# Down stages' first loads in another order, and three neighbours: a kernel for one encoder layer

## The chip, the cores and the metric

The kernel runs on one core of a Trainium2 chip. The metric is the time of one execution on the device in microseconds, as the median of several runs. TensorE (PE) multiplies matrices, VectorE (DVE), ScalarE (ACT) and GpSimd (POOL) work element by element, and SyncE (SP) issues most DMA transfers; ACT issues some as well. Each engine runs its instructions strictly in order: one that waits holds up all that stand behind it on that engine, DMA issues included.

## The reference

One layer of a post-norm encoder is applied to two groups of requests (256 and 512 tokens of 1024 features, 768 tokens in all) with the same weights, in float32:

```python
def swiglu(x, w_gu, w_down):
    gate, up = jnp.split(x @ w_gu, 2, axis=-1)
    return (jax.nn.silu(gate) * up) @ w_down
...
x = layer_norm(DN_ALPHA * x + 0.5 * swiglu(x, ffn1_w_gu[l], ffn1_w_down[l]), ln_g[l, 0], ln_b[l, 0])
x = layer_norm(DN_ALPHA * x + parallel_mixer(...), ln_g[l, 1], ln_b[l, 1])
x = layer_norm(DN_ALPHA * x + memory_cross_attention(x, mem, xa_w_q[l], xa_w_kv[l], xa_w_o[l]), ln_g[l, 2], ln_b[l, 2])
x = layer_norm(DN_ALPHA * x + 0.5 * swiglu(x, ffn2_w_gu[l], ffn2_w_down[l]), ln_g[l, 3], ln_b[l, 3])
```

The hidden width of the two feed-forward layers is 2816. The mixer is a short convolution beside a gated linear attention; the cross-attention reads 256 memory tokens per group, from which it makes keys and values (`k, v = jnp.split(mem @ w_kv, 2, axis=-1)`).

## The kernel before

**Products in three parts.** Each operand of a matrix product is split into a high and a low half (`split`, lines 86 to 88): ACT makes the high half by a conversion (L87, `wh` of a weight tile), DVE or POOL the low one by subtracting it (L88, `wl`). Three matmuls then stand for one: high by high, high by low, low by high. A weight tile so passes through a load into `raw`, a conversion on ACT and a subtraction on DVE before PE can use it.

**A feed-forward layer** (`ffn_fast`, called with n=1 and n=2) has 22 blocks of 128 hidden features. The 768 tokens are two halves of 384, and most blocks use the seven products of Strassen and Winograd in place of eight (`products`). Between them ACT copies a sum out of PSUM (`snap`, L477), so that PE may go on adding to the same bank; PE's next product into that bank waits for that copy. One product is 12 matmuls of 384 columns here. The first two blocks of the first layer, and block 2 of the second, are plain (`plain_block`). At the end of a block `gated` converts h into its halves (`hq`, ACT then DVE), spills them to DRAM (`hspill`), and at every second block makes four sums of h (`hs`, DVE L575 to L578), spilled as well (`sspill`, L582, four DMAs). The last block keeps its h in memory and spills only the sums; those four DMAs are put into a list `late`, which `down_seven` calls.

**The down stage** (`down_seven`, then `down_last`) multiplies h by the second weight matrix. It too is seven products for each of four pairs of blocks, 28 in all, each of 18 matmuls (3 token tiles, 2 steps, 3 parts) of 512 columns. I number them 0 to 27. Products 0 to 7 (P1 and P2) take a quadrant of the weights each and h as it is: 0 and 1 from memory, the others loaded from `hspill` into `ao`, a ring of four buffers. Products 8 to 23 take sums of weight quadrants, made on DVE in the tiles `T` (L331, L337, L346), and sums of h, loaded from `sspill` into `sr` and split into `ao`. The results go into `acc` by additions on DVE (`add`, L294 and L296). `load_acc` loads the three tiles of `acc` that they add to, through ACT's queue (L1215).

A weight quadrant is 512 KB, loaded by `quadrant` (L238). Its place is chosen in `loaded`: of five turns two use tiles of the stage's own pool (`raw7`) and three the ring `raw` of three buffers that all weights of the program share. The stage's pool lies in memory that the last block of the layer still uses, so its tiles come free only at a certain point of that block; the ring does not depend on it. In the program before, turn 1, which is the first product, gets a tile of the pool.

**The order of the work.** The program is written stage by stage, and a scheduler of the framework places each instruction on its engine by the order of the source, the waits and its own estimate. `tc.high_priority()` draws instructions forward, `tc.issue_after(x)` keeps DMAs behind x, and `late_load` keeps loads in the order written. Buffers and completion semaphores add waits: a DMA also waits until the earlier one with the same of eight semaphores has landed. `ahead()` (called near the end of `down_seven`) loads h of the last blocks (`hr`, L653) for `down_last`; it has no bound to how early it may go.

**Keys and values.** While layer norms run on DVE, PE makes the keys for the cross-attention from `w_xk`; the low halves of some weight tiles are made on DVE among the small operations of the layer norm (`rqt`, `rqy`).

Of the kernel before, what the change touches and what calls it, by code (L numbers as in the profile page):

```python
# [26 lines left out]
LO_K = (5, 7)  # L27
# [31 lines left out]
def _encoder(ctx, tc, nc, io, out, dbg):  # L59
# [160 lines left out]

    def down_seven(n, wdn, pairs, keep, dr, sd, order6, load_acc, late, ahead):

        with tc.tile_pool(name=f"seven{n}", bufs=1, reuse_waits="tile") as pool:
            V = nc.vector
            nd = len(pairs)
            raw = [pool.tile([128, 1024], F32, name=nid("raw7")) for _ in range(2)]
            turn = [0]  # L230
            T = {d: pool.tile([128, 1024], F32, name=nid("T")) for d in range(nd)}
# [9 lines left out]
            def loaded(q, d):  # L241
                turn[0] += 1
                if turn[0] % 5 < 2:
                    r = raw[turn[0] % 5]
                else:
                    r = wp.tile([128, 1024], F32, tag="raw", bufs=3, name=nid("raw"))
                quadrant(r[:], q, d)
                return r[:]
# [10 lines left out]
            def direct(t, par, d):  # L259

                if d == 0:
                    return [keep[2 * kp + par][:, t] for kp in pairs[d]]
                a = ring()
                kp = pairs[d][0]
                nc.sync.dma_start(a[:].bitcast(F32), dr[:, t, par, kp:kp + 2])
                return [a[:, k] for k in range(2)]

            def summed(s, d):
                r = pool.tile([128, 2, HT], F32, tag="sr", bufs=3, name=nid("sr"))
                kp = pairs[d][0]  # L270
                nc.sync.dma_start(r[:], sd[:, s, kp:kp + 2])
                a = ring()
                split(a[:, :, 0, :], a[:, :, 1, :], r[:])
                return [a[:, k] for k in range(2)]
# [47 lines left out]
            P1(own[-1])  # L322
            for spill in late:
                spill()
            for d in early:
                quadrant(T[d][:], B11, d)
            load_acc(1, 1)
            add(0, 0, z)
            add(0, 0, x)
            for d in sums_:  # L330
                V.tensor_tensor(T[d][:], T[d][:], loaded(B12, d), op=ALU.add)  # L331
                product(y, summed(0, d), weight(T[d][:]), d == sums_[0], d == sums_[-1])
            load_acc(0, 1)
# [8 lines left out]
            load_acc(1, 0)  # L342
            add(0, 1, y)
            for d in sums_:
                b12, b22 = loaded(B12, d), loaded(B22, d)
                V.tensor_tensor(b12, b12, b22, op=ALU.add)  # L346
                product(x, summed(3, d), weight(b12), False, d == sums_[-1])
            add(1, 1, x)
            ahead()
            for d in own:  # L350
# [58 lines left out]
    def seven(X, pool, more, tt, snap_t, sum_t):  # L409
# [65 lines left out]
        def snap(ps, nm):  # L475
            t = snap_t()
            ins = nc.scalar.activation(t, ps, AF.Copy)  # L477
            if nm == "p1":
                marks["act"] = ins.ins
            return t  # L480
# [6 lines left out]

        def products(b):

            marks["dve_prev"] = marks["dve"]  # L490
            x = psum(nid("px"))[:, :HT]
            product("P1", b, x, True)
            p1 = snap(x, "p1")
            y = psum(nid("py"))[:, :HT]
            product("P5", b, y, True)
            p5 = snap(y, "p5")
            product("P6", b, x, False)
            u2 = snap(x, "u2")
            product("P3", b, y, False)
            up1 = added(y, u2, "up1")  # L500
            product("P7", b, x, False)
            up2 = added(x, p5, "up2")
            z = psum(nid("pz"))[:, :HT]
            product("P2", b, z, True)
            g1 = added(z, p1, "g1")
            product("P4", b, x, False)
            return g1, x, up1, up2
# [3 lines left out]
    def ffn_fast(n, i, front, order6, src, groups, last):  # L511
# [24 lines left out]

        keep = {}

        def block(j, b):
            g1, x, up1, up2 = products(b)  # L540
            h32 = fp.tile([128, TT], F32, tag="h32", bufs=2, name=nid("h32"))
            for half, (g, u) in enumerate(((g1, up1), (x, up2))):
                sil = fp.tile([128, HT], F32, tag="sil", bufs=2, name=nid("sil"))
                nc.scalar.activation(sil[:], g, AF.Silu)  # L544
                ins = nc.vector.scalar_tensor_tensor(h32[:, half * HT:(half + 1) * HT], sil[:], -0.5, u,  # L545
                                                     ALU.mult, ALU.mult)
            marks["dve"] = ins.ins
            gated(j, h32)

        h_of, late = {}, []  # L550

# [7 lines left out]
        def gated(j, h32):  # L559
# [11 lines left out]
            if par and kp not in last:  # L571
                V = nc.vector
                (a11, a21), (a12, a22) = [[h_of[x][:, t, :] for t in range(2)] for x in (j - 1, j)]
                s_ = [glob["hs"].tile([128, HT], F32, tag="hs", bufs=3, name=nid("hs")) for _ in range(4)]
                V.tensor_tensor(s_[3][:], a11, a21, op=ALU.subtract)  # L575
                V.tensor_tensor(s_[0][:], a22, a21, op=ALU.subtract)
                V.scalar_tensor_tensor(s_[1][:], s_[0][:], -1.0, a11, ALU.mult, ALU.subtract)
                V.scalar_tensor_tensor(s_[2][:], s_[1][:], -1.0, a12, ALU.mult, ALU.subtract)  # L578

                def spill():  # L580
                    for x in (3, 0, 1, 2):
                        nc.sync.dma_start(sd[:, x, kp, :], s_[x][:])  # L582

                if j == NFB - 1:
                    late.append(spill)
                else:
                    spill()

# [8 lines left out]

        def plain_block(j, b, before=None):

# [13 lines left out]
            marks["dve"] = ins.ins  # L613
            gated(j, h32)

# [42 lines left out]
        else:  # L658
            lp = hlp.enter_context(tc.tile_pool(name="hlast", bufs=1, reuse_waits="tile"))
            ahead = lambda: load_h(js, lp, "hr", 6)  # L660
        down_seven(n, wdn, groups, keep, dr, sd, order6, load_acc, late, ahead)

# [416 lines left out]
    class Cross:  # L1079
# [22 lines left out]
        def keys_values(self):  # L1102
            s, unit, mh, ml = self.s, self.unit, self.mh, self.ml
            for h in range(4):
                ps = psum(nid("K"))
                for b in range(2):
                    w = load_w(io["w_xk"][2 * h + b], nc.vector if (2 * h + b) in LO_K else None)
                    proj_T(w, s, rh=mh, rl=ml, T=256, ps=ps[:, b * 256:(b + 1) * 256])
                    yield 2650
                a, l = unit("Kh"), unit("Kl")  # L1110
                split(a[:], l[:], ps[:])
                self.Kt.append((a, l))
            for half in range(2):
                pss = [psum(nid("V")) for _ in range(2)]
                for kp in range(4):
                    w = load_w(io["w_xv"][kp, half], nc.vector if kp in LO_V else None)
                    for m in range(2):
# [99 lines left out]
    def front1(env):  # L1217
# [27 lines left out]
        for k in range(4):  # L1245
            sums(X, (env["snap_t"], env["sum_t"]), k, part(k), part(k + 4))
        plain_block(1, w1)
        ip_.close()
# [28 lines left out]
    def front2(env):  # L1277
# [33 lines left out]
        for j in range(2):  # L1311
            env["gated"](j, h01[j])
        env["plain_block"](2, w2)
        return 3, w3
# [133 lines left out]
```

## Time and profile before

| | |
|---|---|
| Median of 3 runs | 1814.77 us (1810.16 to 1815.77) |
| Own time of the profiled execution | 1809.75 us |
| Its span | 1808.0 us |
| Mean granted clock of PE | 0.991 |
| Matmuls | 9758 |
| Moved by DMA | 267.26 MB, mean 148 GB/s |

The times of the trace count from the start of the span. The profiled execution has its own time, which is the span and 1.75 us around it; it lies 5.0 us below the median. A granted clock of 0.5 means that PE runs at half its speed for that time. A timeline's row has start, duration, engine, line, operation, output and inputs, and in brackets the idle time ahead of it and what ended that; "SPq" and "ACTq" are DMA issues in the queues of SP and ACT. A table of waits has the waiting engine and line, the engine and line waited for, the total in us, the number and the longest.

### The profile page before, as it was taken

How to read it: one execution, taken by the hardware profiler on the slowest of the kernel's cores; microseconds unless marked ns; L12 is line 12 of the kernel's file. 1: busy time of each engine (PE TensorE's matmuls, PEld its weight loads, DVE VectorE, ACT ScalarE, POOL GpSimd, SP SyncE). 2: the span in 40 equal slices, each digit the busy share in tenths (PEclk: the TensorE clock that was granted, in tenths of full speed). 3: DMA queues.
4: the chain of work that ended last, by engine and by line, in shares of the span. 5: the costliest groups of instructions: out<-in, count | busy, mean ns of one | idle time of the engine just before them, and what ended most of it. 6: DMA issues, size and time to landing. Idle time of an engine off the chain costs nothing. (4 is left out here: it accounts for less than half of the span.)

```text
span 1808.0 us, 25217 instructions
## 1 busy us (share of the span) xinstructions
PE 1762.3 (97%) x9758; PEld 1618.6 (90%) x9758; DVE 1216.4 (67%) x2035; ACT 763.8 (42%) x1297; POOL 321.7 (18%) x186
## 2 busy tenths in 40 slices
PE   9999999899999999999999999999999999988998
PEld 9999999788889999888888888889899999986886
DVE  8777777377579553577664934585697777754856
ACT  6444454243135544645322244235344444432421
POOL 2000000000224002422244253244430000000012
PEclk9999999899999999999999999999999999998999
DMA  5434333597432333311463252255424343329951
GB/s 193 143 128 157 135 134 104 186 344 253 185 105 94 123 132 125 104 47 41 132 213 117 83 192 66 80 186 176 140 96 154 128 144 131 127 85 346 334 179 70
DMA packets 100535, 267.26 MB, mean 148 GB/s; under 512 B 10016, under 2 KB 23584, under 8 KB 100416
## 3 DMA queue, kind: packets, MB, share of 16 engines
q1 hardware_dynamic: 93504, 250.46, 39.9%
q10 hardware_dynamic: 6912, 15.21, 2.3%
q8 instruction: 76, 1.25, 0.3%
q14 instruction: 43, 0.35, 0.1%
HBM read 212.15 MB, written 53.48 MB: 147 GB/s over the span
## 5 line engine op out<-in xcount | busy, mean ns | idle before, releaser
L88 POOL TENSOR_TENSOR wl<-raw,wh 128x1024 fp32r<-128x1024 f32 (+1 forms) x94 | 231.6, 2468 | 1319.7 <-ACT wh L87 1271.4
L87 ACT ACTIVATE wh<-raw 128x512 fp32r<-128x512 f32 (+2 forms) x309 | 255.5, 830 | 330.0 <-PE to L108 81.6
L88 DVE TENSOR_TENSOR wl<-raw,wh 128x512 fp32r<-128x512 f32 (+2 forms) x215 | 182.8, 853 | 99.6 <-ACT wh L87 99.3
L284 PE MATMUL dn<-wh,ao 128*128 128x512 f32 x600 | 185.4, 389 | 0.0
L106 PE MATMUL pt<-xh,wh 128*128 128x512 f32 (+2 forms) x512 | 173.1, 338 | 0.0
L107 PE MATMUL pt<-xl,wh 128*128 128x512 f32 (+2 forms) x512 | 172.3, 337 | 0.0
L108 PE MATMUL pt<-xh,wl 128*128 128x512 f32 (+2 forms) x512 | 172.0, 336 | 0.0
L284 PEld LDWEIGHTS dn<-wh,ao 128*128 128x128 f32 x600 | 112.6, 188 | 23.5
L87 ACT ACTIVATE wh<-tt 128x512 fp32r<-128x512 f32 x156 | 95.3, 625 | 78.8 <-PE px L472 36.7
L284 PE MATMUL dn<-wl,ao 128*128 128x512 f32 x300 | 116.7, 389 | 0.0
L88 DVE TENSOR_TENSOR wl<-tt,wh 128x512 fp32r<-128x512 f32 x156 | 105.5, 689 | 2.2 <-ACT wh L87 0.5
L106 PEld LDWEIGHTS pt<-xh,wh 128*128 128x128 f32 x512 | 97.0, 189 | 9.7 <-issue 0.5
L108 PEld LDWEIGHTS pt<-xh,wl 128*128 128x128 f32 x512 | 97.0, 189 | 9.0
L107 PEld LDWEIGHTS pt<-xl,wh 128*128 128x128 f32 x512 | 97.1, 190 | 8.8 <-issue 0.2
L472 PE MATMUL px<-xh,wl 128*128 128x384 f32 x232 | 77.5, 334 | 0.0
L472 PE MATMUL px<-xh,wh 128*128 128x384 f32 x232 | 77.5, 334 | 0.0
L472 PE MATMUL px<-xl,wh 128*128 128x384 f32 x232 | 77.5, 334 | 0.0
L545 DVE SCALAR_TENSOR_TENSOR h<-sil,sum 128x384 f32<-128x384 f32 x78 | 43.5, 557 | 47.1 <-ACT sil L544 47.1
L544 ACT ACTIVATE sil<-sum 128x384 f32<-128x384 f32 x39 | 20.5, 526 | 125.9 <-DVE sum L484 125.9
L284 PEld LDWEIGHTS dn<-wl,ao 128*128 128x128 f32 x300 | 56.3, 188 | 11.8
L106 PE MATMUL dn<-wh,hr 128*128 128x512 f32 (+1 forms) x150 | 57.7, 385 | 0.0
L107 PE MATMUL dn<-wl,hr 128*128 128x512 f32 (+1 forms) x150 | 57.5, 383 | 0.0
(374 smaller groups left out, 4866.4 us busy)
## 6 DMA issues: line engine op xcount, KB each, us to landing
raw<-in_ffn_gu_dram SPq DMA_DIRECT2D x84, 512.0 KB, 3.5
raw<-in_ffn_dn_dram SPq DMA_DIRECT2D x64, 512.0 KB, 5.2
hspill<-hq SPq DMA_DIRECT2D x24, 768.0 KB, 3.7
raw<-in_w_mix_dram SPq DMA_DIRECT2D x32, 512.0 KB, 3.5
ao<-hspill SPq DMA_DIRECT2D x18, 768.0 KB, 5.7
sspill<-hs SPq DMA_DIRECT2D x64, 192.0 KB, 2.1
sr<-sspill SPq DMA_DIRECT2D x32, 384.0 KB, 5.7
hr<-hspill SPq DMA_DIRECT2D x24, 384.0 KB, 5.6
```

The source lines that it names most:

```text
L87: nc.scalar.activation(hi, src, AF.Copy)
L88: (lo_eng or nc.vector).tensor_tensor(lo, src, hi.bitcast(F32), op=ALU.subtract)
L106: nc.tensor.matmul(o, lh, rh, start=start, stop=False)
L107: nc.tensor.matmul(o, lh, rl, start=False, stop=False)
L108: nc.tensor.matmul(o, ll, rh, start=False, stop=stop)
L284: nc.tensor.matmul(ps[t][:], l, r[:, o], start=start and k == 0 and m == 0, stop=stop and k == 1 and m == 2, skip_group_check=True)
L472: nc.tensor.matmul(ps, l[:, c], r[:, k, :], start=st and n == 0, stop=sp_ and n == 2, skip_group_check=True)
L544: nc.scalar.activation(sil[:], g, AF.Silu)
L545: ins = nc.vector.scalar_tensor_tensor(h32[:, half * HT:(half + 1) * HT], sil[:], -0.5, u, ALU.mult, ALU.mult)
```

## The change

Four things are changed.

1. In `loaded`, turns 4 and 5 of five use the pool's own tiles, so that the first three loads of a down stage take the shared ring. The re-loads of T for two pairs, with the products of sums behind them, are issued after the last `sr` or `ao` load of the first eight products (`issue_after(last_load)`), and `ahead()` after the last `sr` load of products up to 19.
2. The list `late` is gone: the last block's four spills of sums are issued at their place, on ACT's queue in place of SP's.
3. The h of the last plain block (`gated`) is put into a list and called in the next block behind its first copy (`hooks` in `products`).
4. The loads and conversions of the weights for keys and values stand in `tc.high_priority()`.

```diff
-            turn = [0]
+            turn, last_load = [0], [None]
...
-                if turn[0] % 5 < 2:
-                    r = raw[turn[0] % 5]
+                if turn[0] % 5 in (4, 0):
+                    r = raw[turn[0] % 5 // 4]
...
-            for spill in late:
-                spill()
-            for d in early:
-                quadrant(T[d][:], B11, d)
             load_acc(1, 1)
             add(0, 0, z)
             add(0, 0, x)
-            for d in sums_:
-                V.tensor_tensor(T[d][:], T[d][:], loaded(B12, d), op=ALU.add)
-                product(y, summed(0, d), weight(T[d][:]), d == sums_[0], d == sums_[-1])
+            with tc.issue_after(last_load[0].ins):
+                for d in early:
+                    quadrant(T[d][:], B11, d)
+                for d in sums_:
+                    V.tensor_tensor(T[d][:], T[d][:], loaded(B12, d), op=ALU.add)
+                    product(y, summed(0, d), weight(T[d][:]), d == sums_[0], d == sums_[-1])
...
+            hold = last_load[0].ins
...
-            ahead()
+            with tc.issue_after(hold):
+                ahead()
...
-        def products(b):
+        def products(b, hooks=()):
...
             p1 = snap(x, "p1")
+            while hooks:
+                hooks.pop()()
...
-                def spill():
-                    for x in (3, 0, 1, 2):
-                        nc.sync.dma_start(sd[:, x, kp, :], s_[x][:])
-                if j == NFB - 1:
-                    late.append(spill)
-                else:
-                    spill()
+                queue = nc.scalar if j == NFB - 1 else nc.sync
+                for x in (3, 0, 1, 2):
+                    queue.dma_start(sd[:, x, kp, :], s_[x][:])
...
-            gated(j, h32)
+            if defer:
+                deferred.append(lambda: gated(j, h32))
+            else:
+                gated(j, h32)
...
-                    w = load_w(io["w_xk"][2 * h + b], nc.vector if (2 * h + b) in LO_K else None)
+                    with tc.high_priority():
+                        w = load_w(io["w_xk"][2 * h + b], nc.vector if (2 * h + b) in LO_K else None)
```

The lines of the changed program are shifted by a few: matmuls of the down stage stand at L283, loads of weights at L237, of `ao` at L264, spills at L584. What the scheduler makes of it:

*SP, from the end of the last block of the first layer into its down stage.* Before; `raw7602` holds the weights of product 0, `raw625` those of product 2, `hs597` to `hs600` are the sums of the last block:

```order
L238 DMA raw625_3550<-in_ffn1_dn_dram 128x2x512
L582 DMA sspill1_84<-hs600_3438 128x384
L582 DMA sspill1_84<-hs597_3435 128x384
L582 DMA sspill1_84<-hs598_3436 128x384
L582 DMA sspill1_84<-hs599_3437 128x384
L238 DMA raw7602_3459<-in_ffn1_dn_dram 128x2x512
L265 DMA ao621_3524<-hspill1_83 128x1536
L265 DMA ao624_3548<-hspill1_83 128x1536
L238 DMA T605_3462<-in_ffn1_dn_dram 128x2x512
```

After; `raw615`, `raw618` and `raw621` hold the weights of products 0, 1 and 2, `raw635` those of product 6, `raw7602` now those of product 3:

```order
L237 DMA raw615_3476<-in_ffn1_dn_dram 128x2x512
L237 DMA raw618_3503<-in_ffn1_dn_dram 128x2x512
L584 DMA sspill1_84<-hs541_3139 128x384
L584 DMA sspill1_84<-hs542_3140 128x384
L584 DMA sspill1_84<-hs543_3141 128x384
L237 DMA raw621_3527<-in_ffn1_dn_dram 128x2x512
L237 DMA raw635_3630<-in_ffn1_dn_dram 128x2x512
L264 DMA ao622_3529<-hspill1_83 128x1536
L264 DMA ao625_3553<-hspill1_83 128x1536
L237 DMA raw7602_3463<-in_ffn1_dn_dram 128x2x512
L237 DMA T605_3466<-in_ffn1_dn_dram 128x2x512
```

The four spills of the last block's sums have left SP for ACT, and four weight tiles stand ahead of the first `ao`, where three stood. `ao622` waits for the last of the sums, `hs599`, because it lies where that block's memory was. ACT's and DVE's conversions of `raw615`, `raw618` and `raw621` stand in the last two blocks. In the second layer the same is moved, and the four `hr` loads that stood among the spills ahead of the first `raw` are now near the end of the stage.

*DVE ahead of product 8 of the first layer.* Before; `dn610` to `dn612` are the results of P2, `dn607` to `dn609` those of P1, `wl644` the low weights of product 8:

```order
L331 TENSOR_TENSOR T604_3461<-T604_3461,raw640_3689 128x1024
L88 TENSOR_TENSOR ao642_3694<-sr641_3692,ao642_3694 128x2x384
L331 TENSOR_TENSOR T605_3462<-T605_3462,raw645_3719 128x1024
L296 SCALAR_TENSOR_TENSOR acc_3454<-acc_3454,dn610_3467 128x512
L88 TENSOR_TENSOR wl644_3698<-T604_3461,wh643_3697 128x1024
L296 SCALAR_TENSOR_TENSOR acc_3454<-acc_3454,dn611_3468 128x512
```

After, where these low weights are `wl645`:

```order
L295 SCALAR_TENSOR_TENSOR acc_3458<-acc_3458,dn610_3471 128x512
L295 SCALAR_TENSOR_TENSOR acc_3458<-acc_3458,dn611_3472 128x512
L295 SCALAR_TENSOR_TENSOR acc_3458<-acc_3458,dn612_3473 128x512
L330 TENSOR_TENSOR T604_3465<-T604_3465,raw641_3690 128x1024
L293 TENSOR_TENSOR acc_3458<-acc_3458,dn607_3468 128x512
L293 TENSOR_TENSOR acc_3458<-acc_3458,dn608_3469 128x512
L88 TENSOR_TENSOR ao643_3695<-sr642_3693,ao643_3695 128x2x384
L293 TENSOR_TENSOR acc_3458<-acc_3458,dn609_3470 128x512
L88 TENSOR_TENSOR wl645_3699<-T604_3465,wh644_3698 128x1024
```

All six additions now stand ahead of the low weights, the last of them that of `dn609`, which product 7 completes. The second layer's stage reads the same.

*DVE at the first wait for keys.* Before, with `wl1443` the low weights that PE waits for:

```order
L142 TENSOR_TENSOR rqt1408_9247<-rqy1407_9246 128x1
L142 TENSOR_TENSOR rqt1414_9272<-rqy1413_9271 128x1
L88 TENSOR_TENSOR xl_3450<-lt1417_9303,xh_3449 128x4x128
L143 SCALAR_TENSOR_TENSOR rqt1408_9247<-rqt1408_9247,rqa1405_9244 128x1
L143 SCALAR_TENSOR_TENSOR rqt1414_9272<-rqt1414_9272,rqa1411_9269 128x1
L88 TENSOR_TENSOR xl_3450<-lt1418_9310,xh_3449 128x4x128
L144 SCALAR_TENSOR_TENSOR rqy1407_9246<-rqt1408_9247,rqy1407_9246 128x1
L144 SCALAR_TENSOR_TENSOR rqy1413_9271<-rqt1414_9272,rqy1413_9271 128x1
L88 TENSOR_TENSOR wl1443_9480<-raw1441_9478,wh1442_9479 128x1024
```

After, where the same weights are `wl1444`:

```order
L88 TENSOR_TENSOR wl1444_9481<-raw1442_9479,wh1443_9480 128x1024
L142 TENSOR_TENSOR rqt1409_9248<-rqy1408_9247 128x1
L142 TENSOR_TENSOR rqt1415_9273<-rqy1414_9272 128x1
L88 TENSOR_TENSOR xl_3454<-lt1418_9304,xh_3453 128x4x128
L143 SCALAR_TENSOR_TENSOR rqt1409_9248<-rqt1409_9248,rqa1406_9245 128x1
```

The weights have moved ahead of eight operations. At the second wait for keys they pass one addition into `acc`. On ACT, where the h of the plain block stands ahead of the next block's first copy, the rows are the same in both programs: `hq`, then `snap`.

More of the change, by code (lines that the diff above doesn't have):

```diff
@@ L219, in down, with down_seven @@
             tok_mm(ps, w, kk, hh[s.name, t, j], hl[s.name, t, j], first and kk == 0, stop and kk == 1, cols)
-    def down_seven(n, wdn, pairs, keep, dr, sd, order6, load_acc, late, ahead):
+    def down_seven(n, wdn, pairs, keep, dr, sd, order6, load_acc, ahead):
         with tc.tile_pool(name=f"seven{n}", bufs=1, reuse_waits="tile") as pool:
@@ L264, in direct @@
                 kp = pairs[d][0]
-                nc.sync.dma_start(a[:].bitcast(F32), dr[:, t, par, kp:kp + 2])
+                last_load[0] = nc.sync.dma_start(a[:].bitcast(F32), dr[:, t, par, kp:kp + 2])
                 return [a[:, k] for k in range(2)]
@@ L270, in summed @@
                 kp = pairs[d][0]
-                nc.sync.dma_start(r[:], sd[:, s, kp:kp + 2])
+                last_load[0] = nc.sync.dma_start(r[:], sd[:, s, kp:kp + 2])
                 a = ring()
@@ L535, in weights @@
             return weights_of(wgu[j], wgu[NFB + j])
-        keep = {}
+        keep, deferred = {}, []
         def block(j, b):
-            g1, x, up1, up2 = products(b)
+            g1, x, up1, up2 = products(b, deferred)
             h32 = fp.tile([128, TT], F32, tag="h32", bufs=2, name=nid("h32"))
@@ L548, in block @@
             gated(j, h32)
-        h_of, late = {}, []
+        h_of = {}
         def hq_tile(hs):
@@ L596, in plain_weights, with plain_block @@
             return [x for x, _ in b]
-        def plain_block(j, b, before=None):
+        def plain_block(j, b, before=None, defer=False):
             ps = {(g, t): psum(nid("pp"))[:, :HT] for g in range(2) for t in range(2)}
@@ L660, in ffn_fast @@
             ahead = lambda: load_h(js, lp, "hr", 6)
-        down_seven(n, wdn, groups, keep, dr, sd, order6, load_acc, late, ahead)
+        down_seven(n, wdn, groups, keep, dr, sd, order6, load_acc, ahead)
         with tc.tile_pool(name=f"down{n}", bufs=1, reuse_waits="tile") as f2:
@@ L1115, in keys_values @@
                 for kp in range(4):
-                    w = load_w(io["w_xv"][kp, half], nc.vector if kp in LO_V else None)
+                    with tc.high_priority():
+                        w = load_w(io["w_xv"][kp, half], nc.vector if kp in LO_V else None)
                     for m in range(2):
@@ L1246, in front1 @@
             sums(X, (env["snap_t"], env["sum_t"]), k, part(k), part(k + 4))
-        plain_block(1, w1)
+        plain_block(1, w1, defer=True)
         ip_.close()
@@ L1312, in front2 @@
             env["gated"](j, h01[j])
-        env["plain_block"](2, w2)
+        env["plain_block"](2, w2, defer=True)
         return 3, w3
```

## The prediction

> **What bounds the kernel now.** The page comes first, its head, the row of PE and the rows of slices for PE, the granted clock and the DMA engines.
>
> ```profile
> span 1808.0 us, 25217 instructions
> PE 1762.3 (97%) x9758; PEld 1618.6 (90%) x9758; DVE 1216.4 (67%) x2035; ACT 763.8 (42%) x1297; POOL 321.7 (18%) x186
> ...
> PE   9999999899999999999999999999999999988998
> ...
> PEclk9999999899999999999999999999999999998999
> DMA  5434333597432333311463252255424343329951
> ```
>
> PE is the bound: 97% busy. Its dips ahead of the tail (the slice from 316 us and the two from 1582) stand where the two stretches begin in which the DMA engines are fullest. The share says nothing of what can be won; the waits of PE do, so they come next.
>
> ```profile
> PE dn L284 <- ACT wh L87: 20.8, 2, 11.9
> PE px L472 <- ACT snap L477: 4.3, 2, 3.5
> PE K L108 <- DVE wl L88: 4.0, 2, 2.3
> ```
>
> Three waits, and the change speaks to all of them: the first product of each down stage, the copy in the block after the plain one, and the weights of the keys. The timeline of PE places them; the bracket is the idle time before a row.
>
> ```profile
> 43.39 0.33 PE L472 MATMUL py<-S1l,wh 128*128 128x384 f32 x1
> 43.56 0.34 PE L472 MATMUL py<-S1h,wl 128*128 128x384 f32 x1
> 47.35 0.69 PE L472 MATMUL px<-S2h,wh 128*128 128x384 f32 x1 [3.46 <-ACT snap L477]
> ...
> 335.90 0.34 PE L472 MATMUL px<-A22h,wl 128*128 128x384 f32 x1
> 345.11 1.22 PE L284 MATMUL dn<-wh,hq 128*128 128x512 f32 x2 [8.87 <-ACT wh L87]
> ...
> 1633.31 1.22 PE L284 MATMUL dn<-wh,hq 128*128 128x512 f32 x2 [11.92 <-ACT wh L87]
> ```
>
> ACT's conversion is named, but it is not what comes late. The timelines of SP's queue, ACT and DVE at the first stage:
>
> ```profile
> 323.63 16.65 SPq L582 DMA_DIRECT2D sspill<-hs  x4
> 340.39 0.38 SPq L238 DMA_DIRECT2D raw<-in_ffn_dn_dram  x1
> 340.89 0.89 SPq L265 DMA_DIRECT2D ao<-hspill  x2
> ...
> 344.00 1.06 ACT L87 ACTIVATE wh<-raw 128x1024 fp32r<-128x1024 f32 x1 [5.70 <-DMA raw<-in_ffn_dn_dram]
> ...
> 345.08 1.23 DVE L88 TENSOR_TENSOR wl<-raw,wh 128x1024 fp32r<-128x1024 f32 x1 [5.15 <-ACT wh L87]
> ```
>
> The load of the first weights is issued at 340.39, after four spills that hold SP's queue for 16.65 us, and ACT starts when it has landed, 3.6 us later. At the second stage four loads of h stand ahead as well:
>
> ```profile
> 1621.28 0.81 SPq L653 DMA_DIRECT2D hr<-hspill  x2
> 1623.19 2.25 SPq L582 DMA_DIRECT2D sspill<-hs  x3
> 1625.48 0.94 SPq L653 DMA_DIRECT2D hr<-hspill  x2
> 1626.76 0.38 SPq L238 DMA_DIRECT2D raw<-in_ffn_dn_dram  x1
> ```
>
> What the stall costs beyond the idle time, and how full the DMA engines are behind it, is read from a table of stretches (after PE's busy time come PEld, DVE, ACT and POOL; the last three columns are granted clock, DMA share and GB/s):
>
> ```profile
> 345.10:352.40 7.30, 7.25 (x19) 5.28 (x20) 5.18 (x5) 4.01 (x4) 0.00 (x0) 0.59 1.02 398
> 352.40:361.00 8.60, 8.60 (x39) 7.03 (x38) 3.20 (x3) 2.27 (x3) 0.00 (x0) 1.00 0.90 341
> 372.00:381.00 9.00, 9.00 (x41) 7.48 (x40) 7.70 (x10) 4.44 (x5) 0.00 (x0) 1.00 1.01 384
> 1633.30:1640.00 6.70, 6.65 (x19) 4.85 (x20) 4.71 (x4) 3.92 (x4) 0.00 (x0) 0.65 1.03 411
> 1640.00:1664.00 24.00, 24.00 (x107) 19.77 (x106) 7.06 (x7) 5.07 (x6) 0.00 (x0) 1.00 0.94 345
> ```
>
> After each stall PE computes its first product at a mean clock of 0.59 and 0.65. At full clock 107 matmuls take 24.00 us, so a product of 18 takes 4.04 us.
>
> **The change part by part.** *First products.* The three earliest weight tiles, and the one for product 6, now use buffers that come free before the last block ends, so they are loaded and converted ahead; the spills leave SP's queue for ACT's, and in the second stage the loads of h go behind. The first two products take h that is still in memory, so nothing else holds them. Gone are 8.87 and 11.92 us idle, and at half clock 7.30 x (1 - 0.59) = 3.0 and 6.70 x (1 - 0.65) = 2.3 us: **26.1 us**.
>
> *What is late next.* PE reaches product p of the first stage at 336.15 + 4.04p. Product 2 needs `ao`, which is issued only after the last sum of h:
>
> ```profile
> 339.39 0.55 DVE L578 SCALAR_TENSOR_TENSOR hs<-hs,h 128x384 f32<-128x384 f32 x1
> ...
> hspill<-hq SPq DMA_DIRECT2D x24, 768.0 KB, 3.7
> ao<-hspill SPq DMA_DIRECT2D x18, 768.0 KB, 5.7
> sspill<-hs SPq DMA_DIRECT2D x64, 192.0 KB, 2.1
> hr<-hspill SPq DMA_DIRECT2D x24, 384.0 KB, 5.6
> acc<-in_x_tok_dram ACTq DMA_DIRECT2D x12, 256.0 KB, 5.9
> ```
>
> Issued at 340.0, it lands between 343.7 (the 3.7 us of an equal transfer on a quiet core) and 345.7 (its own median in the crowd), wanted at 344.2: from nothing to 1.5 us. I take 0.7, since only small transfers run beside it. Product 3's weights follow two `ao` and must be converted (1.06 us): 0 to 2, I take 0.8. In the second stage the first `ao` no longer waits for the sums; I take 0.3 for product 3, of 0 to 1.
>
> Product 8 has a new wait of its own. Its low weights stood behind one addition into `acc`, and now stand behind all six, the last of which needs the end of product 7. Two rows of DVE give the price:
>
> ```profile
> 376.54 0.68 DVE L296 SCALAR_TENSOR_TENSOR acc<-acc,dn 128x512 f32<-128x512 f32 x1
> 377.13 1.22 DVE L88 TENSOR_TENSOR wl<-T,wh 128x1024 fp32r<-128x1024 f32 x1
> ```
>
> 0.68 + 1.22 = 1.9 us after product 7, less three matmuls (0.7) that PE can do with the high half first: 1.2, with the semaphores 1.3 us per stage, and 0.2 for product 9. Queued behind it on DVE are the sums for products 9 to 11; each takes some 3.4 us of DVE against 4.04 of PE, so DVE catches up. New waits: 0.7 + 0.8 + 1.5 = 3.0 in the first stage, 0.3 + 1.5 = 1.8 in the second, **4.8 us** (1 to 13, by the bounds here and the transfers below).
>
> *Do the transfers follow?* From 340.0 to product 8's weights there pass 6 `ao`, 7 weight tiles of 512 KB, 5 `acc` and 3 spills, 10.3 MB. At 384 GB/s that is 26.8 us; with 2.2 us until the first bytes arrive (3.6 less 1.3 for 512 KB) they land at 369.0, and the sum and the conversion end at 371.3. Wanted is 336.15 + 32.3 + 1.5 = 370.0: 1.3 us, which the wait on DVE covers already. At the 341 GB/s of the stretch from 352.4 it is 374.6, a wait of 4.6. I take the higher rate, because in the slower stretch SP waited for PE to free `ao` buffers, which now happens earlier. In the second stage one `ao` is early and four loads of h (1.6 MB, 4 us) are out of the way, so it has room.
>
> The Trainium skill (DMA: Bandwidth & Descriptors, Specifications) gives some 358 GB/s as the limit of a core's HBM reads, and (Issuing engines are not separate DMA queues) says that another issuing engine adds no bandwidth. Here 398 and 411 GB/s are measured, mixed with other traffic; by the page's figure an estimate for product 8 is 373.3, a wait of 3.3 instead of 1.3 us.
>
> *ACT and DVE in the last blocks.* Three conversions of 1.06 and 1.23 us move in there. At the tightest place one stands ahead of a copy that PE wants one product later, 12 matmuls at 0.17 = 2.08 us; conversion and copy (0.48, below) take 1.6 of it. Nothing, with 0.5 us to spare; without that cover up to 0.5 in each of six places, 3 us. ACT's queue now waits for the sums with its spills, but the next conversion behind them needs weights that land after 347 anyway.
>
> *Keys and values.* DVE's rows at the two waits:
>
> ```profile
> 1031.45 0.21 DVE L142 TENSOR_TENSOR rqt<-rqy 128x1 f32<-128x1 f32 x2
> ...
> 1033.05 1.22 DVE L88 TENSOR_TENSOR wl<-raw,wh 128x1024 fp32r<-128x1024 f32 x1
> ...
> 1203.13 1.41 DVE L177 SCALAR_TENSOR_TENSOR acc<-acc,rqy,ln_b 128x512 f32<-128x512 f32 x2
> 1204.46 1.22 DVE L88 TENSOR_TENSOR wl<-raw,wh 128x1024 fp32r<-128x1024 f32 x1
> ```
>
> At the first, the conversion moves from 1033.05 to where 1031.45 stands: 1.6 us of the wait. At the second it passes one of two additions, 0.7. Together **2.3 us** (0 to 4.0, the whole row of waits; not below nothing, as what it passes is not what PE waits for).
>
> *The deferred h.* ACT decides this wait:
>
> ```profile
> 46.08 0.84 ACT L87 ACTIVATE hq<-h 128x768 fp32r<-128x768 f32 x1 [1.62 <-DVE h L611]
> 46.83 0.47 ACT L477 ACTIVATE snap<-px 128x384 f32<-128x384 f32 x1
> ```
>
> The copy that PE wants stands behind `hq`. In the changed program it still does, row for row, so this part is worth **nothing** and the 3.46 us stay.
>
> **The sum** is -26.1 + 4.8 - 2.3 = -23.6 us. The profiled execution took 1809.75 (its span 1808.0 and 1.75 around it), 5.0 below the median of the runs shown. The mean of it and the three runs is 1812.6, and from there the forecast is **1789.0**; from the profiled execution it would be 1786.2, from the median 1791.2.
>
> **The rivals.** *The transfers bind.* Against the forecast, the DMA share is 0.90 to 1.02 through the first eight products, so PE catches up with the stream: 4.6 us at product 8 of the first stage and some 2 at each of the two before and after it, and 4 to 5 in the second; 15 us of new waits in place of 4.8, which gives 1799. For the forecast speaks that SP's queue waited for PE in between. Chance 0.22.
>
> *The clock falls at the new waits* (the slower side). Place: products 2, 3 and 8 of both stages. The smallest gap after which the trace shows half clock is the 3.46 us above; the next below it, 2.3 us at the keys, lies in a slice that the page gives as 9, full. A wait past that point costs 3.46 and the 3.0 of a first product at half clock, 6.5 us; six of them, 39, turn the gain of 28.4 into a loss: 1823. Five give 1816.7, still no measurable difference; it decides only from six on. The sums above put each wait under 2 us. Chance 0.04. The Trainium skill (TensorE: Matmul & The Clock Gate, Part 1) puts the point at an idle window of about 3.4 us, with which the row agrees.
>
> *The loads are not early.* If SP still holds them behind a wait of the last block (the load for product 6 waits for a conversion there), only the keys' 2.3 remain: 1810. The conversions are placed inside the last block, which speaks against it. Chance 0.06.
>
> *Nothing new is late, and the deferred h acts after all*: 26.1 + 4.0 + 3.46 gone, 1779. Chance 0.06, since the order of ACT shows it unmoved.
>
> **How the numbers follow.** The forecast has 0.62, with its own range from 1782 (no new wait, keys wholly gone: -30.1) to 1795. About 0.3%, 5.4 us, is what a measurement of this kernel can tell from no change. Faster are the forecast, the bound by transfers and the best case, 0.90; same 0.06; slower 0.04. The range 1780 to 1802 takes in forecast and transfers with a few us for the run-to-run spread, and leaves out the rest.
>
> **What would show it.** Right: PE's row of waits for `dn` falls from 20.8 to under 6 us, no clock below 1 at the starts of the down stages, and at product 8 PE waits for DVE's `wl` some 1.3 us. The keys' row falls to about 1.7; the 3.46 us for `snap` stay. The transfers bind if PE's waits at products 2 to 11 name conversions that themselves wait for DMA, with the share at 1.0 throughout. Wrong outright, if the first product of a stage still waits for a load.

## The result, and the profile after

The changed kernel takes 1791.62 us (median of 4 runs, 1790.31 to 1793.5) against 1813.39 (4 runs, 1810.16 to 1815.77) for the kernel before: a ratio of 0.9882, 95% interval [0.9862, 0.9902], 21.8 us less. The forecast was 1789.0, range 1780 to 1802. The profiled execution took 1790.79 us, 19.0 less than that of before; it lies 0.8 us below the median of its kernel, that of before 3.6 us below its own.

The page's head, PE's slices and the granted clock:

```profile
span 1789.0 us, 25220 instructions
PE 1759.3 (98%) x9758; PEld 1615.0 (90%) x9758; DVE 1218.3 (68%) x2035; ACT 763.9 (43%) x1297; POOL 321.0 (18%) x186
...
PE   9999999999999999999999999999999999999998
...
PEclk9999999999999999999999999999999999999999
```

The dips at the two down stages are gone, in PE's share and in its clock. PE's waits in the profile after:

```profile
PE px L473 <- ACT snap L478: 4.2, 2, 3.4
PE dn L283 <- DVE wl L88: 3.0, 3, 1.3
PE K L108 <- DVE wl L88: 2.6, 1, 2.6
...
PE dn L283 <- DMA ao<-hspill: 1.5, 1, 1.5
PE to L106 <- ACT xh L87: 1.5, 1, 1.5
...
PE dn L283 <- ACT wh L87: 0.9, 1, 0.9
...
PE pT L1174 <- DVE e L1163: 0.4, 1, 0.4
```

The 20.8 us of `dn` for the first weights have become three smaller rows of 5.4 in all; the row of `snap` stands as it was; the row of the keys has one wait in place of two, and that one is longer than either was (2.6 against 2.3). The timeline of PE says where the new waits are:

```profile
335.75 0.34 PE L473 MATMUL px<-A22h,wl 128*128 128x384 f32 x1
335.92 0.39 PE L283 MATMUL dn<-wh,hq 128*128 128x512 f32 x1
...
344.12 0.39 PE L283 MATMUL dn<-wh,hq 128*128 128x512 f32 x1
346.02 0.50 PE L283 MATMUL dn<-wh,ao 128*128 128x512 f32 x1 [1.51 <-DMA ao<-hspill]
...
351.24 0.96 PE L283 MATMUL dn<-wh,ao 128*128 128x512 f32 x3 [0.86 <-ACT wh L87]
352.50 0.50 PE L283 MATMUL dn<-wl,ao 128*128 128x512 f32 x1 [0.30 <-DVE wl L88]
...
374.55 0.50 PE L283 MATMUL dn<-wl,ao 128*128 128x512 f32 x1 [1.34 <-DVE wl L88]
...
1649.84 0.50 PE L283 MATMUL dn<-wl,ao 128*128 128x512 f32 x1 [1.34 <-DVE wl L88]
```

The down stage follows the last block without a gap. Product 2 waits for its `ao`, product 3 for its weights, and product 8, in both stages, for the low half. Each wait costs a little more than its idle time: from 344.12 to 346.02 are 1.90 us, where the next matmul usually starts 0.23 later.

DVE ahead of product 8 shows the mechanism that the forecast had priced:

```profile
371.21 0.69 DVE L293 TENSOR_TENSOR acc<-acc,dn 128x512 f32<-128x512 f32 x1 [0.30 <-PE dn L283]
371.81 0.95 DVE L88 TENSOR_TENSOR ao<-sr,ao 128x768 fp32r<-128x768 f32 x1
372.68 0.68 DVE L293 TENSOR_TENSOR acc<-acc,dn 128x512 f32<-128x512 f32 x1
373.28 1.22 DVE L88 TENSOR_TENSOR wl<-T,wh 128x1024 fp32r<-128x1024 f32 x1
```

The addition of 372.68 needs the end of product 7; behind it come the low weights, ready at 374.50.

### The profile page after: what moved, and what is told of

Same layout as the page of the kernel before. It is cut to its first block, busy times and chain, and to the rows that moved or that the text cites. A ratio compares the mean times of both kernels' runs of the same rounds, so it can differ in the third digit from the quotient of the medians.

```text
span 1789.0 us, 25220 instructions
## 1 busy us (share of the span) xinstructions
PE 1759.3 (98%) x9758; PEld 1615.0 (90%) x9758; DVE 1218.3 (68%) x2035; ACT 763.9 (43%) x1297; POOL 321.0 (18%) x186
## 5 line engine op out<-in xcount | busy, mean ns | idle before, releaser
L283 PE MATMUL dn<-wh,ao 128*128 128x512 f32 x600 | 185.9, 390 | 2.4 <-DMA ao<-hspill 1.5
L283 PEld LDWEIGHTS dn<-wh,ao 128*128 128x128 f32 x600 | 112.6, 188 | 26.4 <-DMA ao<-hspill 1.9
L283 PE MATMUL dn<-wl,ao 128*128 128x512 f32 x300 | 117.5, 392 | 3.0 <-DVE wl L88 3.0
L283 PEld LDWEIGHTS dn<-wl,ao 128*128 128x128 f32 x300 | 56.3, 188 | 16.9 <-DVE wl L88 5.2
L547 ACT ACTIVATE sil<-sum 128x384 f32<-128x384 f32 x39 | 20.5, 525 | 118.8 <-DVE sum L485 118.8
```

Of the source, the lines that this page charges most:

```text
L283: nc.tensor.matmul(ps[t][:], l, r[:, o], start=start and k == 0 and m == 0, stop=stop and k == 1 and m == 2, skip_group_check=True)
```

## The experiments

Ratios are to the kernel before, with their 95% intervals. The first four ran in one session, the next three with the changed kernel itself (e0) in a second, the last three in a third; the kernel before had medians of 1812.9, 1812.7 and 1812.3 in them.

**What freed the first product: the buffers or the queue?** The old choice of buffers in the changed kernel:

```diff
-                if turn[0] % 5 in (4, 0):
-                    r = raw[turn[0] % 5 // 4]
+                if turn[0] % 5 < 2:
+                    r = raw[turn[0] % 5]
```

> The changed kernel with the old choice of buffers: turns 1 and 5 take the stage's own tiles, so the first product's weights lie again where the last block's memory was. Theory (what held the first load was SP's queue, blocked 16.65 us by spills): the spills are still on ACT's queue, so the load is issued when that memory comes free, some 6 us before the block's end, and lands in time. PE's wait at the first product of each stage stays under 1 us; with one tile fewer loaded ahead the transfers press more, 0 to 6 us more than the changed kernel, 1791 to 1798. Rival (the place of the buffer decides): the first product waits as before, some 9 to 12 us in each stage and half clock behind it, 1810 to 1817.

Measured: 1804.59 us (1802.69 to 1806.18), 0.9958 [0.9942, 0.9973], between the two ranges. PE waits 5.2 us at the first product of each stage. The load in SP's queue:

```profile
330.28 0.38 SPq L237 DMA_DIRECT2D raw<-in_ffn_dn_dram  x1
```

and ACT, which converts it:

```profile
337.67 0.84 ACT L87 ACTIVATE hq<-h 128x768 fp32r<-128x768 f32 x1 [0.62 <-DVE h L548]
338.25 2.27 ACTq L584 DMA_DIRECT2D sspill<-hs  x3
340.57 1.06 ACT L87 ACTIVATE wh<-raw 128x1024 fp32r<-128x1024 f32 x1 [2.06 <-DMA sspill<-hs]
```

The load is issued at 330.28 and has landed, by the trace, at 333.9, in time, as the theory said. Its conversion is not: on ACT it stands behind the last `hq` and the three spills, which wait for the sums there. The spills were not removed by the second edit, they were moved to the queue of the engine that converts. Both readings were half right: SP's queue held the load, and without early buffers ACT's queue holds the conversion.

**The spills back on SP**, with the new buffers:

```diff
-                queue = nc.scalar if j == NFB - 1 else nc.sync
+                queue = nc.sync
```

> The changed kernel with the last block's spills back on SP's queue, at their place in the program. Theory (either edit takes the load out from behind the spills): the first three weight tiles are issued ahead of the spills, the first load of h waits for the last sum in any case, so nothing changes but some 0.3 us at product 2: 1791 to 1793. Rival (the queue alone decides, so both edits are needed): 10 to 26 us slower, 1801 to 1817.

Measured: 1795.01 (1794.68 to 1798.87), 0.9905 [0.9888, 0.9921]. The theory's mechanism holds for the first three tiles, as no product 0 or 1 waits; its 0.3 us at product 2 do not. PE's waits:

```profile
PE dn L283 <- DMA ao<-hspill: 6.6, 2, 3.7
```

Two stretches of the table by windows, which has the granted clock in the third column from the right:

```profile
346.20:349.50 3.30, 2.83 (x7) 2.25 (x8) 0.00 (x0) 0.00 (x0) 0.00 (x0) 0.50 1.04 418
1629.70:1632.90 3.20, 3.20 (x9) 2.52 (x8) 0.00 (x0) 0.60 (x1) 0.00 (x0) 0.50 1.05 424
```

Product 2 waits 2.9 us in the first stage, where it was 1.5, and 3.7 in the second, where it was nothing: there the first `ao` stands behind the spills again. PE runs at half clock behind both. So the spills' move is worth 5.1 us of waits at product 2 and the half clock behind them; 1.2 us go the other way, since product 3 of the first stage no longer waits. The time does not show it: the median lies 1.0 us above that of the changed kernel's repeat (e0 below), and the intervals overlap.

**The choice of buffers alone**, in the kernel before:

```diff
-                if turn[0] % 5 < 2:
-                    r = raw[turn[0] % 5]
+                if turn[0] % 5 in (4, 0):
+                    r = raw[turn[0] % 5 // 4]
```

> The kernel before with the new choice of buffers alone: spills on SP, nothing held back by issue_after, no priority, nothing deferred. Theory: the first product's stall goes in both stages, but two weight tiles of products 8 and 9 and three loads of h stand ahead of the first ao in SP's queue, so product 2 waits some 3 us longer than in the changed kernel, 4 to 5 us, past the point at which the clock halves: 6 to 9 us worse than the changed kernel in the first stage and 0 to 6 in the second, 1798 to 1806. Rival (the choice of buffers is the whole gain): 1791 to 1794.

Measured: 1800.69 (1797.67 to 1801.56), 0.9933 [0.9918, 0.9949], in the theory's range. This row stands where the 20.8 us stood:

```profile
PE dn L284 <- DMA ao<-hspill: 8.5, 2, 4.3
```

The first products do not wait, product 2 waits 4.2 and 4.3 us. The small edit takes a little over half of the gain (12 of 22 us). The rest comes back two products later, and the spills' move (e2) is part of what prevents that; what the two `issue_after` do by themselves was not tried.

**No priority for keys and values** (the two `with tc.high_priority():` taken out):

> The changed kernel without the priority for keys and values. Theory: PE's waits for the keys go back from 2.6 to about 4.0 us; the changed kernel gained 1.6 at the first wait and lost 0.3 at the second, so this one is 1 to 1.5 us slower, which no time can show but the table of waits can: 1791 to 1794. Rival (priority costs as much elsewhere in the cross-attention as it gains at the keys): the waits for keys go back and the end of the keys and values stage stands at the same distance from the end of the first layer's down stage within 0.5 us.

Measured: 1795.13 (1792.03 to 1797.33), 0.9905 [0.9887, 0.9922]. The waits answer:

```profile
PE K L108 <- DVE wl L88: 4.0, 2, 2.2
```

They go back to 4.0, as in the kernel before. The rival's sign is not met: counted from the first matmul of the keys, the changed kernel is 1.2 us ahead at the end of the values. What it says comes a stage later. In the attention that follows the changed kernel gives 1.1 us back: PE waits there for DVE's `e` (0.4) and starts later. In the changed kernel's repeat (e0 below) the scores lose nothing, but half clock behind the keys takes the gain. From that first matmul to the last of the scores' transposes (`pT`) PE takes 251.8 us in the first profile of the changed kernel, 251.9 in its repeat and 251.9 without priority, so nothing is left of the 1.2. The medians tell nothing of this: e3 lies 3.5 us above the changed kernel's first median and 1.1 above its second, and in its profile PE ran 10.2 us of the mixer at half clock, which the first profile of the changed kernel did not.

**The changed kernel again:**

> The changed kernel once more, as the base of the three below on the same chip: 1790 to 1794. The clock is looked at: so far PE ran at half clock for 3.41 us at a time after gaps of 1.1 to 3.4 us in some executions and not in others, the gap being the same. If chance decides, the places of half clock differ again from the first profile, while the gaps above 1 us stay where they were, within 0.3 us.

Measured: 1794.03 (1792.11 to 1795.2), 0.9896 [0.9881, 0.9911]. The gaps stand where they were, within 0.3 us (3.27, 1.36, 0.89, 1.34, 1.54, 1.12, 2.47, against 3.36, 1.51, 0.86, 1.34, 1.54, 1.12, 2.60). Behind the gaps of 1.12 and 2.47 PE now ran at half clock, for 6.83 and 3.41 us. The same gap has half clock behind it in one execution and not in another, as expected; what tells them apart is in the last section.

**The deferred h held back in earnest:**

```diff
             while hooks:
-                hooks.pop()()
+                with tc.issue_after(marks["act"]):
+                    hooks.pop()()
```

> The changed kernel with the deferred h really held behind the next block's first copy on ACT (issue_after on that copy). Theory (the copy is late because hq stands ahead of it): PE's wait for snap in the first layer falls from 3.4 to about 1 us, since the copy then starts at the end of the second sil, and the half clock behind it goes: 2.4 + 1.6 = 4 us; in the second layer two waits of 0.85 go too, 1.7 us at most. 1785 to 1788. Rival (hq is then late itself, and with it the next block's operands on ACT): waits for operands of the same size appear in the next block, 1790 to 1794.

Measured: 1790.98 (1787.78 to 1793.3), 0.9874 [0.9858, 0.9891]. ACT after the first plain blocks:

```profile
45.10 0.49 ACT L478 ACTIVATE snap<-px 128x384 f32<-128x384 f32 x1
46.83 0.85 ACT L87 ACTIVATE hq<-h 128x768 fp32r<-128x768 f32 x1 [1.24 <-DVE h L609]
...
48.62 0.47 ACT L478 ACTIVATE snap<-py 128x384 f32<-128x384 f32 x1
```

The copy now stands ahead of `hq`, and PE waits 0.93 us for it in place of 3.36. `hq` then delays the conversions behind it and with them the second copy: a new wait of 1.13. The half clock is gone. The profile is 2.6 us ahead of that of e0 at the first down stage; in the second layer one wait of 0.82 goes and the other stays (1.00). Theory and rival both take part: the median is 3.1 us below that of e0, where the theory had 4 to 5.7. The time alone does not tell it from e0, since the intervals overlap.

**The low weights of product 8 first** (`low[0]` is the subtraction that `weight` issued last):

```diff
-            add(0, 0, x)
...
                     product(y, summed(0, d), weight(T[d][:]), d == sums_[0], d == sums_[-1])
+                    if d == sums_[0]:
+                        with tc.issue_after(low[0]):
+                            add(0, 0, x)
```

> The changed kernel with the three additions of the P1 results put behind the low weights of product 8 on DVE. Theory (the six additions ahead cause the 1.34 us at product 8 and the small waits at 9): both go in both stages, 2 x 1.5 = 3 us less, 1787 to 1790. Rival (the transfers are the next thing that is late, by at most 0.9 us the slack of the high half): the wait changes its name to a conversion or a load and keeps 1 us, 1790 to 1793.

Measured: 1791.67 (1789.87 to 1794.95), 0.9886 [0.9871, 0.9901]. PE at product 8 of both stages, and at product 24 of the second:

```profile
372.64 0.50 PE L283 MATMUL dn<-wl,ao 128*128 128x512 f32 x1 [0.30 <-DVE wl L88]
...
1650.00 0.50 PE L283 MATMUL dn<-wl,ao 128*128 128x512 f32 x1 [0.81 <-DVE wl L88]
1715.99 0.47 PE L283 MATMUL dn<-wh,hq 128*128 128x512 f32 x1 [1.10 <-DVE acc L293]
```

The wait shrinks from 1.34 to 0.30 and 0.81, and what is gained comes back at product 24, which now waits for a late addition (0.60 in the first stage, 1.10 in the second): 2.8 us in all, where it was 2.7. The additions caused the wait; putting them elsewhere only moves it. The median is 2.4 us below that of e0, with overlapping intervals, and the waits do not explain that.

**The first loads of `acc` later:**

```diff
-                if d == 0:
+                if d == 2:
                     load_acc(0, 0)
```

> The changed kernel with the first three loads of acc (768 KB in all) issued two pairs later. Theory (they share the DMA engines with the first ao, which lands 6.1 us after its issue): at 380 GB/s they take 2 us, so the wait of 1.5 us at product 2 goes, and of the 0.9 + 0.3 at product 3 at least half: 2 us in the first layer's stage, at most 0.3 in the second, 1788 to 1791. Rival (the two ao share the engines with each other and the weights behind them, and the spills): the wait at product 2 keeps 1 us or more.

Measured: 1797.24 (1795.34 to 1798.2), 0.9913 [0.9899, 0.9928]. The median is 3.2 us above that of e0; no run of the one lies among those of the other, though the intervals overlap. The wait at product 2 is gone, and so is the 0.86 at product 3: the theory of the shared engines was right there. Then product 8:

```profile
372.06 0.96 PE L283 MATMUL dn<-wh,ao 128*128 128x512 f32 x3 [1.67 <-ACT wh L87]
373.84 0.79 PE L283 MATMUL dn<-wl,ao 128*128 128x512 f32 x1 [0.82 <-DVE wl L88]
```

and DVE ahead of it:

```profile
368.73 1.23 DVE L330 TENSOR_TENSOR T<-T,raw 128x1024 f32<-128x1024 f32 x1 [1.69 <-DMA raw<-in_ffn_dn_dram]
```

DVE waits for the weights of product 8; high and low half are late by 1.67 and 0.82 in the first stage, and by 1.84 and 0.80 in the second, with half clock behind both. Counted from the start of the first stage these weights land, by the trace, at 32.2 us, 0.7 later than in the profile after, and PE is ready for product 8 some 2.6 us sooner, because it no longer waits at products 2 and 3. This is the forecast's rival, the bound by transfers, and PE runs into it mostly by coming early. The waits of the two stages are 5.4 us in all, as before; the half clock behind product 8 (6.83 and 3.41 us) is new.

**The last two edits that lowered the median, e4 and e5, and the keys on DVE.** The third is

```diff
-LO_K = (5, 7)
+LO_K = (5, 6, 7)
```

> Both edits that helped together: h pinned behind the first copy, and the low weights of product 8 ahead of the additions. Theory (they are 300 us apart and add): 3 and 2.4 us below the changed kernel's 1794.0 of the same session, 1787 to 1790. Rival (half clock after small gaps, which falls by chance, is larger than either): 1789 to 1793, with two or more stretches of 3.41 us at half clock in the profile.

> The changed kernel with one more weight tile of the keys subtracted on DVE in place of POOL, the one whose subtraction (2.40 us on POOL, from 1192.08) ran beside two additions into acc that took 3.58 us together where they take 1.41 elsewhere. Theory (DVE is held while POOL subtracts, and that is why the second wait for the keys did not shrink): the additions take 1.4 us again and the wait of 2.6 falls under 1 us; 1 to 2 us in the time, 1790 to 1794. Rival (DVE's own queue is too long there): the additions take 1.4 us and the wait keeps 2 us or more, since DVE got 1.2 us more to do.

> The two edits and the tile on DVE together. Theory: another 1 to 2 us below the first of these three, 1785 to 1789. Rival: no difference from it within 1.5 us.

Measured: e10 1789.5 (1787.04 to 1791.46), 0.9873 [0.9858, 0.9889]; e12 1789.98 (1789.32 to 1790.48), 0.9877 [0.986, 0.9893]; e13 1785.42 (1782.39 to 1786.67), 0.9849 [0.9833, 0.9865]. e10 lies in both of its ranges; the three stretches of half clock in its profile are its rival's sign, and it beats each single edit by less than the sum. In e12 PE has no wait for the keys left. DVE and POOL in the changed kernel (two rows) and in e12 (two rows):

```profile
1191.45 3.58 DVE L177 SCALAR_TENSOR_TENSOR acc<-acc,rqy,ln_b 128x512 f32<-128x512 f32 x2
...
1192.08 2.40 POOL L88 TENSOR_TENSOR wl<-raw,wh 128x1024 fp32r<-128x1024 f32 x1 [1.65 <-ACT wh L87]
```

```profile
1192.08 3.24 DVE L88 TENSOR_TENSOR wl<-raw,wh 128x1024 fp32r<-128x1024 f32 x1
...
1191.83 2.41 POOL L88 TENSOR_TENSOR wl<-raw,wh 128x1024 fp32r<-128x1024 f32 x1 [14.73 <-ACT wh L87]
```

The additions take 1.41 again in e12, yet DVE meets another subtraction of POOL: the low weights of 1.22 us take 3.24, from the start of POOL's to 1.1 us past its end. DVE is held while POOL subtracts; that half of the theory holds. The other half, that this is why the second wait did not shrink, is not shown by it: another row was moved as well, since the order puts the last keys' low weights ahead of two additions, so the wait's end is not the collision's doing alone. e13, with all three, lies below every run of both kernels, its interval apart from that of e0, which ran a session earlier; PE's profile has no half clock there but at the end. It is 4.1 us below e10, where the theory had 1 to 2; how much of that is half clock is not told apart.

## Why the prediction was right

*The first products* were sized at 26.1 us, and PE's stall and its half clock went in full: the stage follows the block without a gap, in both layers. With the matmuls of the two profiles lined up in order, PE gains 26.6 us there. The cause was told in half. The forecast read the spills in SP's queue as what held the load; e1 shows that with the queue cleared and the old buffers 5.2 us stay at each stage, behind the same spills on ACT. The early buffers are what lets the conversions pass them.

*Product 8* was predicted at 1.3 us in each stage and measured at 1.34 in both, from two rows of the profile before and the order. *Product 3* was put at 0.8 and has 0.86 + 0.30 in the first stage; the 0.3 in the second did not come. *Product 2* was put at 0.7 and has 1.51, the upper end: its `ao` was issued at 339.85 and landed, by the trace, 6.1 us later, where the forecast had 3.7 to 5.7. The choice of the low value failed on its ground, "only small transfers run beside it": e8 shows that the loads of `acc` are what make it late. In all 4.8 us were put against 5.4 idle and some 1.6 for restarting, of which the forecast counted only the 0.2 at product 9 of each stage: from 344.12 to 346.02 are 1.90, less 0.23 for the usual step and 1.51 idle 0.16, and the following step takes 0.34 instead of 0.23. That is some 0.27 for each of five waits; product 9 loses 0.13 in each stage.

*Keys*: the step that failed. 2.3 us were forecast; PE's waits fell by 1.4, and behind the scores nothing of it was left (e3). The first wait went, as forecast. The second was to fall by 0.7 and grew by 0.3. Its low weights did pass an addition, but the two additions ahead of it met POOL's subtraction (3.58 in place of 1.41). That is only a part of it, for in the kernel before the same subtraction held DVE too, just ahead of the rows that the forecast read:

```profile
1200.42 0.69 DVE L88 TENSOR_TENSOR Kl<-K,Kh 128x512 fp32r<-128x512 f32 x1
1201.02 1.88 DVE L143 SCALAR_TENSOR_TENSOR rqt<-rqt,rqa 128x1 f32<-128x1 f32 x1
...
1200.48 2.40 POOL L88 TENSOR_TENSOR wl<-raw,wh 128x1024 fp32r<-128x1024 f32 x1 [2.48 <-ACT wh L87]
```

An operation that usually takes 0.16 took 1.88 there. So 2.17 us lost to POOL stand against 1.72, which is 0.45 of the 1.0 us that the forecast was off; for the rest no cause is shown.

*The deferred h* was worth nothing, as forecast from the order: its wait is 3.36 after 3.46. Pinned, the same idea lowers the median by 3.1 us (e4), with overlapping intervals.

*The conversions in the last blocks* cost nothing, as forecast: no wait of PE appears there.

*The transfers* leave little room. The forecast had product 8's weights landing at 369.0; by the trace they landed at 367.4, and DVE's sum of them started at 369.09, behind an addition, without waiting for them. The room is 1.7 us, and in e8 it is used up. The Trainium skill's 358 GB/s (DMA: Bandwidth & Descriptors, Specifications) would have made this wait 3.3 us; the stretches of e2 with 418 and 424 GB/s decide against it as a limit of this run. Its statement that another issuing engine adds no bandwidth agrees with the profile after: from 350 to 360, with loads of SP's queue alone under way, the DMA engines moved 392 GB/s, and from 360 to 370, with three loads of ACT's queue beside them, 389.

*The rival of the clock* had its point at 3.46 us. The runs put it far lower (below). It did not decide because the waits were few and short, not because they stayed under the point: behind the five new ones, of 1.51 us at most, neither profile of the changed kernel shows half clock.

The sum for the profiled executions: -26.1, + 7.0 for the new waits, - 1.4 at the keys, + 1.4 in the attention and the mixer's output (`xh`, 0.8 to 1.5, and `e`) is -19.1; measured 19.0. Lined up matmul by matmul, PE gains 26.6 us at the two first products and loses 7.5 behind them, which comes to -19.1 as well. The 21.8 between the medians are larger because the profiled execution of before lies further below its median; what the other executions of before lost is not on record. By the medians the forecast came closer than by its terms: from the profiled execution it was 1786.2, and the changed kernel's took 4.6 us more, 2.2 at the new waits, 0.9 at the keys and 1.4 in the attention and the mixer's output, which the forecast put at nothing.

## What to carry to other kernels

A load that waits in a queue has a conversion behind it that waits in another: when a blocker is moved from one queue to another, ask what stands behind it there. A wait that was priced from the instruction order and two durations came out within 0.1 us at product 8; at the second wait for keys the same way was 1.0 us off, since another engine's work changed the durations. One that is priced from the crowd of transfers needs the list of what is in flight. Once PE runs through, the next limits lie within 1 to 2 us of each other (DVE's additions, `acc`, weights), and taking one away shows the next (e5, e8). So edits are best tried together: of e4, e5 and e12 none has an interval apart from that of e0, and the three together have.

## What the runs showed of the hardware

**Half clock after small gaps.** PE's row after a gap of 1.54 us, from the timeline of the changed kernel:

```profile
826.27 0.93 PE L904 MATMUL kv<-acc,kT 64*128 64x128 f32 x11 [1.54 <-DVE uc L973]
```

and the stretches around it in the table by windows:

```profile
821.81:825.22 3.41, 2.92 (x30) 2.55 (x28) 2.23 (x4) 2.15 (x4) 0.00 (x0) 1.00 0.24 96
825.22:828.63 3.41, 2.36 (x28) 2.20 (x29) 3.27 (x8) 3.06 (x7) 0.18 (x3) 1.00 0.00 0
```

The same gap in e4:

```profile
824.09 2.25 PE L905 MATMUL kv<-acc,kT 64*128 64x128 f32 x21 [1.54 <-DVE uc L974]
```

and the stretches around it:

```profile
821.21:824.62 3.41, 1.87 (x26) 1.68 (x24) 3.19 (x5) 2.62 (x5) 0.18 (x3) 1.00 0.00 0
824.62:828.03 3.41, 3.41 (x24) 3.09 (x21) 2.83 (x9) 2.32 (x7) 0.00 (x0) 0.50 0.00 0
```

Behind the gap the clock is 1.00 in one and 0.50 in the other. In the profiles of this case stretches at half clock last 3.41 us or a multiple of it, the one at the end apart. They start whole steps of 3.413 us apart: in e4 at 824.62, 869.00 and 1200.09, which are 13 and 97 steps. So there is a grid that is fixed within an execution, and from one execution to another it lies elsewhere against the program. The stretches above are steps of these grids. In e4 the gap fell whole into one step; in the changed kernel a border cut it into 0.49 and 1.05.

The other profiles bear this out, with exceptions. The gap of 1.54 fell whole into one step in six of the thirteen, with half clock behind it in all six; it was cut in seven, with half clock in one of them (e5, cut into 1.24 and 0.30). At the keys and at `snap`, gaps of 2.2 to 3.5 us had half clock behind them in all fourteen cases in which one step held 1.98 us or more of the gap, and in none of the seven with at most 1.87, the 3.01 us of e2 (1.20 and 1.81) among them. What looks like chance is then where the grid lies. Why less is enough in the mixer than at the keys is not shown.

A stretch of 6.83 us cost e0 some 3.0 us against the first profile of the changed kernel (870 to 878), so a stretch costs up to half its length. Profiles had from none (e13) to five (e8, 20.5 us in all) of them ahead of the end, and the time goes with the mean clock: the four executions of e4 took 1793.3, 1791.63, 1790.34 and 1787.78 us at clocks of 0.995, 0.995, 0.996 and 0.998. This explains most of the spread between runs of one kernel. The Trainium skill (TensorE: Matmul & The Clock Gate, Part 1) has the gate watch a free-running window of some 3.4 us; the grid agrees with that. Its rule that only gaps above some 3.4 us are to be avoided is not borne out here.

**DVE held by POOL.** Operations of DVE on two operands in SBUF that meet a subtraction on POOL are held until POOL has ended: 3.24 us in place of 1.22 in e12, and 1.88 in place of 0.16 in the kernel before. There `Kl<-K,Kh`, which reads one operand from PSUM, ran beside the same subtraction in its usual 0.69. The Trainium skill (SBUF — State Buffer, Who interferes with whom) has the two engines share a pair of ports as an exclusive lock, and says that a DVE instruction with two inputs in SBUF contends with a POOL instruction that reads SBUF; the rows agree.
